# The MLP's up projection in seven products for eight, ahead of the whole down projection

## The chip, the cores and the metric

The kernel runs on one core of one Trainium2 chip, and the other cores are idle. The metric is the device time of one execution in microseconds. A core has TensorE (PE, matrix products out of SBUF into the eight banks of PSUM), VectorE (DVE, elementwise), ScalarE (ACT, elementwise functions of one operand), GpSimd (POOL, elementwise, no access to PSUM) and SyncE (SP, which issues the DMAs). Each engine works through its own queue in order, and semaphores tie the queues together.

## The reference

One layer of a decoder is computed for 544 tokens: a prompt of 512 and 8 samples of 4 new tokens. The width is 2048 and the MLP's hidden width 8192. All arrays are fp32.

```
x = x + concat(gla_part, att_part) @ w_out
h = rmsnorm(x, ffn_norm_w)
x = x + square(relu(h @ w_up)) @ w_down
y = rmsnorm(x, final_norm_w)
```

Ahead of this stand one combined projection, a gated linear attention, a dilated window attention, and the updates of their states. Only the output projection (`w_out`), the MLP (`w_up` of 2048 x 8192 and `w_down` of 8192 x 2048) and the last normalization matter here.

## The kernel before

Activations lie transposed, 128 features on the partitions and 544 tokens along the row, so that one tile `b` is 128 x 544. Matmuls take the tokens in two halves of 272 (`half`, L298). A matmul of this kernel runs in the reduced type fp32r, and full precision comes from splitting: every operand is a high part (rounded by ACT) and a low part (the remainder, a subtraction on DVE), and a product is three matmuls, high by high, high by low and low by high. For activations `put_x` (L367) makes the two parts, for weights `split_w` (L234): the tile `raw` of 128 x 1024 arrives by DMA, and each half of it, 128 x 512, becomes `wh` and `wl`. There are three buffers of each of `raw`, `wh` and `wl` (`NRAW`, `NWH`, L45).

The order of the work is the order of the program. The weights stand in one list `W`; `preps` is the list of the splits, and `prep_to` (L218) runs them some two or three steps ahead of the matmuls. `slot_main` (L1074) does one weight tile of 8 chunks: it starts the load of the tile three further on, splits, runs 48 matmuls into two banks and calls an evacuation. `defer` and `begin` (L317) put work at the start of a later slot, and `post` is a list of small pieces of work, of which one is run in each step.

The output projection has 32 slots. Behind each pair of them `evac_wo` (L1160) adds the residual, splits the scaled sum into the operand `X2` of the up projection and keeps its squares for the norm. Beside it run 32 updates of the recurrent state on DVE, one per slot (`start_upd`, L1200).

The MLP goes by eight groups of 1024 hidden features. A group's up projection is eight blocks of 128 features, each of two slots or 96 matmuls (16 chunks, three terms, two halves). `evac_up` (L1303) takes the relu and the factor of the norm out of PSUM on DVE, and ACT squares. The down projection of the first seven groups is already in the seven products of Winograd's form of Strassen's algorithm: the hidden blocks are combined into seven operands as they are made (`xops`, L1273), the weights into sums (`pair_preps`, L250; two of the four sums on POOL), and `down_pair` (L1324) runs seven products of 12 matmuls, each in a bank of its own out of eight, with ten additions on DVE into four running sums per pair of output blocks (`acc`). The next group's first up block is put between (`up_blocks`, L204). The last group's down projection is plain, 32 blocks of 24 matmuls, by halves of the tokens, with the last norm's squares beside it; `finish_acc` (L1351) turns the running sums into the result on POOL, during the last group's up projection.

Of the kernel before, what the change touches and what calls it, by code (L numbers as in the profile page):

```python
# [6 lines left out]
F32 = mybir.dt.float32  # L7
# [40 lines left out]
NSLOT3 = 9  # L48
SUMS = 5
# [72 lines left out]
def _body(ctx, nc, tc, A):  # L122
# [22 lines left out]
    def alloc(dt=F32):  # L145
        cnt[0] += 1
        n = f"b{cnt[0]}"
        for free, p, tag, bufs in tiers:
            if free[0]:
                free[0] -= 1  # L150
                t = p.tile([128, NTOK], dt, name=n, tag=tag, bufs=bufs)
                home[id(t)] = (t, free)
                return t
        raise SystemExit(f"no slots at {slot[0]}")
# [11 lines left out]

    def fix_done():
        fixctx.close()
        tiers.append(([NSLOT3], ctx.enter_context(tc.tile_pool(name="sb3", bufs=NSLOT3, side="right")), "blk3", NSLOT3))
# [29 lines left out]
    wo_seq = [(0, 0), (1, 0), (0, 1), (1, 1)]  # L199
    for nb in range(2, 16):  # L200
        wo_seq += [(nb, 0), (nb, 1)]
    for nb, hf in wo_seq:
        W.append(A["wout"][nb, hf])
    def up_blocks(g):  # L204
        """The up projections before group g's down projections: the next group's first one keeps TensorE busy while
        the operands of the last one are made."""
        return [(g, n) for n in range(g > 0, 8)] + ([(g + 1, 0)] if g < 7 else [])

    paired = set()
    for g in range(8):  # L210
        for g2, n in up_blocks(g):
            W += [A["wup"][g2 * 8 + n, hf] for hf in range(2)]
        if g < 7:
            paired.update(range(len(W), len(W) + 16, 2))
        W += [A["wdn"][g, nb % 16] for nb in range(32 if g == 7 else 16)]
# [18 lines left out]
    def split_w(key, r, eng):  # L234
        h = whm[key] = pool.tile([128, 4, 128], R32, name="wh%d_%d" % key, tag="wh", bufs=NWH)
        l = wlm[key] = pool.tile([128, 4, 128], R32, name="wl%d_%d" % key, tag="wl", bufs=NWH)
# [9 lines left out]
    def sum_tile():  # L246
        t = alloc()
        return t, t[:, :512].rearrange("p (c n) -> p c n", c=4)

    def pair_preps(i):  # L250
        """Weights of two blocks of output features, cut in halves by feature and by contraction, for the seven
        products of Winograd's form of Strassen's algorithm."""
        v = {}

        def a(r, q):
            return raws[i + r][:, 4 * q:4 * q + 4, :]

        def sm(k, x, y, op):
            t, v[k] = sum_tile()
            (G if SUMS >> (k - 1) & 1 else V).tensor_tensor(v[k], x, y, op=op)  # L260
            v[-k] = t

        def take(u, k):
            split_w((i, u), v[k], V)
            rel(v[-k])

        def u0():
            split_w((i, 0), a(0, 0), V)
            sm(1, a(1, 0), a(1, 1), OP.add)
            sm(2, v[1], a(0, 0), OP.subtract)  # L270

        def u1():
            split_w((i, 1), a(0, 1), V)
            sm(4, a(0, 1), v[2], OP.subtract)
            sm(3, a(0, 0), a(1, 0), OP.subtract)
            load_to(i + NRAW + 1)

        def u6():
            split_w((i, 6), a(1, 1), V)
            load_to(i + NRAW + 2)  # L280

        return [u0, u1, lambda: take(2, 4), lambda: take(3, 1), lambda: take(4, 3), lambda: take(5, 2), u6]

# [5 lines left out]
    while i < len(W):  # L289
        uidx[i] = len(preps)  # L290
        if i in paired:
            preps += pair_preps(i)
            i += 2
        else:
            preps += [lambda i=i: split_q(i, 0), lambda i=i: split_q(i, 1)]
            i += 1
# [852 lines left out]
    X2 = [None] * 16  # L1149
    xr = {}  # L1150

    def xr_load(nb):
        if nb < 16:
            xr[nb] = alloc()
            nc.sync.dma_start(xr[nb], A["xT"][nb])

    ss2 = alloc()
    r2 = alloc()

    def evac_wo(nb):  # L1160
        def f(pb):
# [3 lines left out]
            a, b = alloc(R32), alloc(R32)  # L1165
            put_x(a, b, t, nw[:, 16 + nb:17 + nb])
            X2[nb] = (a, b)
# [11 lines left out]
            defer(1, st_)  # L1179
        return f  # L1180
# [19 lines left out]
    def start_upd():  # L1200
# [5 lines left out]
        for k in range(32):  # L1206
            fetch, update, put = state_upd(k // 8, k % 8, *bufs[k % NUB])
            defer(k, fetch)
            defer(k + UD, update)
            defer(k + NUB - 1, put)  # L1210
        defer(31 + NUB, lambda: (rel(*own), fix_done()))

    xr_load(0)
    xr_load(1)
    wpb = {}
    base = n_in
    for s, (nb, hf) in enumerate(wo_seq):
        if hf == 0:
            wpb[nb] = mpair()
        if hf == 1 and nb == 0:  # L1220
            drain(lambda: all(n in GO for n in range(8)), gens)
            for n in range(8):
                put_go(n)
            defer(SUD, start_upd)
        slot_main(base + s, wpb[nb], Y, 8 * hf, hf == 0, hf == 1, evac=evac_wo(nb) if hf else None, nbg=2)
        if hf == 1:
            xr_load(nb + 2)
        elif nb == 0:
            pass
    for a, b in Y:  # L1230
        rel(a, b)
    base += len(wo_seq)
    begin()
    slot[0] += 1
    begin()

    acc = [alloc() for _ in range(16)]
    rel(GW["a"], GW["w"])

    x2t = {}  # L1240

# [4 lines left out]
    b0, b1 = balloc(), balloc()  # L1246
    r2done = [False]
    ah = [None] * 8
    perm = (0, 2, 4, 6, 1, 3, 5, 7)
    prev = {}  # L1250
    held = []
    xop = {k: [None] * 4 for k in ("B11", "B21", "B22", "T1", "T2", "T3", "T4")}

    def new_x():
        t = alloc(R32), alloc(R32)
        held.extend(t)
        return t

    def parts(names, j, src):
        t = new_x()  # L1260
        put_x(t[0], t[1], src)
        for hf, k in enumerate(names):
            xop[k][j] = (half(t[0], hf), half(t[1], hf))

    def first_op(j):
        a = prev["a"]
        if j % 2 == 0:
            prev["b"] = new_x()
        h, l = (half(t, j % 2) for t in prev["b"])
        xop["B11"][j] = (h, l)  # L1270
        post.append(lambda: put_x(h, l, half(a, 0)))

    def xops(n, a):  # L1273
        """The seven operands of a pair of hidden blocks (halves of the contraction) and the two halves of the tokens."""
        j = n // 2
        if n % 2 == 0:
            prev["a"] = a
            if n:
                first_op(j)
            return  # L1280
        a1, a2 = prev["a"], a

        def mix():
            ta = alloc()
            V.tensor_sub(half(ta, 0), half(a1, 1), half(a1, 0))
            V.tensor_sub(half(ta, 1), half(a2, 1), half(a1, 1))
            rel(a1)
            tb = alloc()
            V.tensor_sub(half(tb, 0), half(a2, 1), half(ta, 0))
            V.tensor_sub(half(tb, 1), half(a2, 0), half(tb, 0))  # L1290
            rel(a2)
            post.insert(0, lambda: (parts(("T2", "T4"), j, tb), rel(tb)))
            post.insert(0, lambda: (parts(("T1", "T3"), j, ta), rel(ta)))

        post.append(lambda: parts(("B21", "B22"), j, a2))
        post.append(mix)

    def split_a(n, t):
        ah[n] = (alloc(R32), alloc(R32))
        put_x(ah[n][0], ah[n][1], t)  # L1300
        rel(t)

    def evac_up(g, n):  # L1303
        def f(pb):
            if not r2done[0]:
                rms_r(r2, [ss2], D, (b0, b1))
                rel(ss2)
                brel(b0, b1)
                r2done[0] = True
            t = alloc()  # L1310
            for hf in range(2):
                V.scalar_tensor_tensor(half(t, hf), pb[hf][:, :HALF], 0.0, half(r2, hf), op0=OP.max, op1=OP.mult)
            S.activation(t, t, AF.Square)
            if g < 7 or n == 0:
                xops(n, t)
            else:
                split_a(n, t)
        return f

    # The sums kept are C11, C12 - C22, C21 - C22 and C22, to which the products go without sums of their own.  # L1320
    STEPS = (("B11", ((0, 0, 1), (1, 1, 1))), ("B21", ((0, 0, 1),)), ("B22", ((0, 1, 1),)),
             ("T1", ((1, 1, 1), (1, 0, 0))), ("T3", ((1, 1, 1), (0, 1, 0))), ("T2", ((1, 1, 1),)), ("T4", ((1, 0, 1),)))

    def down_pair(i, p):  # L1324
        for u, (x, outs) in enumerate(STEPS):
            if u % 3 == 0:
                begin()
# [237 lines left out]
```

## Time and profile before

| what | value |
|---|---|
| timed runs | 2416.05, 2418.59 and 2419.27 us, median 2418.59 |
| span of the profiled execution, first to last instruction | 2414.2 us |
| median less that span | 4.4 us |
| output projection, by the timeline | about 724 to 932 us |
| MLP, by the timeline | about 932 to 2399 us |
| DMA in the MLP | 104 GB/s |

The page of a profile gives busy times by engine, the chain of work that ended last, and groups of instructions by line. All of the kernel's instructions pass through one helper, so that the line is L94 nearly everywhere, and the names of the tiles tell them apart: `bank` is PSUM, `b` an activation tile (and here also a sum of weights), `raw`, `wh`, `wl` the weights. `out<-in` names what is written and read; `PEld` is TensorE's load of the stationary operand, one for each matmul. In a timeline a row has the start, the length, the engine, the operation, the count of instructions that it merges, and in brackets how long the engine was idle before and who released it. A row of a stretch has the busy time of each engine with its instructions, then the granted clock, the share of the DMA engines and GB/s.

### The profile page before, as it was taken

The page shows a single profiled execution, that of the slowest core. Times are in us where ns is not written, and L with a number is a line of the kernel's source. Part 1 is how long each engine was busy: PE and PEld are TensorE (multiplying, and loading weights), DVE is VectorE, ACT ScalarE, POOL GpSimd, SP SyncE. Part 2 cuts the span into 40 slices and gives each one's busy share as a digit, 9 for nine tenths or more (in the row PEclk, how much of TensorE's full clock was granted, in tenths as well). Part 3 has the DMA queues.
Part 4 walks back from the last instruction along what each step waited for, and adds up shares of the span by engine and source line. Part 5 has one row for each costly group of instructions (what it writes and reads, how often), then busy time and mean ns, then how long its engine had stood idle before and what let it go on. Part 6 is the DMA issues. An engine that isn't in the chain of part 4 may idle for free.

```text
span 2414.2 us, 47201 instructions
## 1 busy us (share of the span) xinstructions
PE 2383.4 (99%) x18836; PEld 2357.8 (98%) x18836; DVE 1776.7 (74%) x3589; ACT 911.7 (38%) x1680; POOL 564.2 (23%) x385
## 2 busy tenths in 40 slices
PE   9999999999999999999999999999999999999997
PEld 8999999999999999999999999999999999999997
DVE  6988888888876777476488488488487488488556
ACT  5332333332344323344333333333333333333365
POOL 3554544333431110021021021021021021022501
PEclk9999999999999999999999999999999999999999
DMA  6776765455525776223223223223223223223445
GB/s 231 272 261 246 261 230 183 174 192 191 176 82 170 265 262 229 88 84 103 89 86 105 88 87 107 89 86 106 89 89 106 89 86 107 90 85 123 144 157 179
DMA packets 116088, 355.30 MB, mean 147 GB/s; under 512 B 13051, under 2 KB 26363, under 8 KB 115868
## 3 DMA queue, kind: packets, MB, share of 16 engines
q1 hardware_dynamic: 114716, 351.18, 42.7%
q8 instruction: 147, 2.41, 0.4%
q10 hardware_dynamic: 1152, 1.11, 0.1%
q14 instruction: 73, 0.60, 0.1%
HBM read 334.02 MB, written 18.22 MB: 146 GB/s over the span
## 4 chain that ended last, share of the span: by engine, by line
PE 87%; DVE 8%; issue 2%; ACT 1%; DMA 1%; SPq 0%; DVEq 0%; ACTq 0%
PE bank L94 87%; DVE b L94 6%; DVE wl L94 1%; ACT b L94 1%; ACT wh L94 0%; DMA raw<-wup 0%; DVE AT L94 0%; DMA kv<-kcg 0%; DVE kv L94 0%; DMA b<-wglr 0%; DMA b<-xT 0%; DMA raw<-wdn 0%; DMA vtok<-s 0%; ACT L984 0%; DVE st L94 0%
## 5 line engine op out<-in xcount | busy, mean ns | idle before, releaser
L94 PE MATMUL bank<-b,wh 128*128 128x272 f32 x11648 | 1619.6, 288 | 2.8 <-ACT wh L94 1.4
L94 PEld LDWEIGHTS bank<-b,wh 128*128 128x128 f32 x11648 | 1522.1, 188 | 5.5 <-ACT wh L94 3.4
L94 PE MATMUL bank<-b,wl 128*128 128x272 f32 x5824 | 902.4, 291 | 0.0
L94 PEld LDWEIGHTS bank<-b,wl 128*128 128x128 f32 x5824 | 791.5, 189 | 8.7 <-issue 3.9
L94 ACT ACTIVATE wh<-raw 128x512 fp32r<-128x512 f32 x732 | 454.0, 627 | 624.1 <-PE bank L94 541.3
L94 DVE TENSOR_TENSOR wl<-raw,wh 128x512 fp32r<-128x512 f32 x552 | 411.5, 753 | 299.0 <-PE bank L94 205.2
L94 ACT ACTIVATE b<-b 128x544 f32<-128x544 f32 (+8 forms) x389 | 220.2, 572 | 412.0 <-DVE b L94 399.4
L94 POOL TENSOR_TENSOR wl<-raw,wh 128x512 fp32r<-128x512 f32 x180 | 270.6, 1509 | 384.3 <-ACT wh L94 330.2
L94 POOL TENSOR_TENSOR b<-raw 128x512 f32<-128x512 f32 x56 | 76.9, 1374 | 1095.6 <-ACT wh L94 628.1
L94 DVE TENSOR_TENSOR b<-b,b 128x272 f32<-128x272 f32 (+9 forms) x429 | 236.4, 574 | 38.3 <-ACT b L94 33.3
L94 DVE TENSOR_TENSOR wl<-b,wh 128x512 fp32r<-128x512 f32 x224 | 194.2, 867 | 35.6 <-ACT wh L94 35.0
L94 DVE TENSOR_TENSOR b<-b,bank 128x272 f32<-128x272 f32 x528 | 213.6, 427 | 1.9 <-PE bank L94 0.3
L94 ACT ACTIVATE wh<-b 128x512 fp32r<-128x512 f32 x224 | 135.1, 628 | 183.1 <-DVE b L94 129.6
L94 DVE SCALAR_TENSOR_TENSOR b<-bank,b 128x272 f32<-128x272 f32 (+1 forms) x228 | 90.7, 439 | 143.8 <-PE bank L94 135.5
L94 POOL TENSOR_TENSOR b<-b,b 128x544 f32<-128x544 f32 (+2 forms) x73 | 101.9, 1404 | 351.6 <-ACT b L94 293.3
L94 DVE SCALAR_TENSOR_TENSOR kv<-kv,b 128x320 f32<-128x320 f32 x256 | 159.2, 680 | 3.6 <-DMA kv<-vcg 3.6
L94 PE MATMUL bank<-b,b 128*128 128x272 f32 (+5 forms) x712 | 101.4, 311 | 6.0 <-ACT b L94 6.0
L94 DVE SCALAR_TENSOR_TENSOR b<-kv,b,b 128x320 f32<-128x320 f32 x126 | 100.1, 795 | 0.0
L94 POOL TENSOR_TENSOR b<-raw,raw 128x512 f32<-128x512 f32 x56 | 96.8, 1729 | 0.0
L94 PEld LDWEIGHTS bank<-b,b 128*128 128x128 f32 (+2 forms) x712 | 83.4, 177 | 12.1 <-ACT b L94 6.3
L94 DVE SCALAR_TENSOR_TENSOR b<-kv,b 128x320 f32<-128x320 f32 x126 | 93.5, 742 | 2.3 <-DMA kv<-kcg 2.2
L94 ACT ACTIVATE b<-bank 128x512 f32<-128x512 f32 (+5 forms) x114 | 44.6, 421 | 129.2 <-PE bank L94 101.7
(71 smaller groups left out, 749.5 us busy)
## 6 DMA issues: line engine op xcount, KB each, us to landing
raw<-wdn SPq DMA_DIRECT2D x144, 512.0 KB, 3.3
raw<-wup SPq DMA_DIRECT2D x128, 512.0 KB, 3.3
raw<-win SPq DMA_DIRECT2D x90, 512.0 KB, 4.8
kv<-kcg SPq DMA_DIRECT2D x64, 640.0 KB, 4.8
kv<-vcg SPq DMA_DIRECT2D x64, 640.0 KB, 4.9
raw<-wout SPq DMA_DIRECT2D x32, 512.0 KB, 5.8
b<-xT SPq DMA_DIRECT2D x32, 272.0 KB, 5.4
b<-vs SPq DMA_DIRECT2D x32, 256.0 KB, 5.1
```

The costliest lines, as they stand in the source:

```text
L94: return f(*a, **k)
```

## The change

The up projection goes into seven products as well, and the whole of it comes ahead of the down projection.

Operands of the up projection. The 16 blocks of its input are combined in pairs `j`, `j + 8` into seven operands per pair, each of half the tokens (`up_b2`, `up_b1`, `up_ta`, `up_tb`). To this end the output projection takes its blocks in the order 0, 8, 1, 9 and so on. The first three pairs of operands (`NEARLY = 3`) are made as `post` work during the output projection, the other five inside the first eight units of the up projection.

Units. The MLP is now a list of units of 12 matmuls. A pair of hidden blocks is seven products of two units; there are 32 pairs, and P4 of a pair stands behind P2 of the next. `run` prepares the weights two units ahead, then runs one piece of `post` or the unit's own `before`, the matmuls, and `after`. Weight tiles have seven buffers (`NRAW2 = 4` more), and `wh` and `wl` three as before. All sums of weights, four per seven products, are on DVE.

PSUM. Products that end in the same sum are accumulated in the same bank, one behind the other, and the bank is read in between where an intermediate sum is needed.

Hidden blocks. The relu moves to ACT and loses the factor of the norm, which is squared (`r2_calc`, in the second pair) and multiplied in at the end. The operands of the down projection are made from each pair at once and written to DRAM, seven tiles of 128 x 544 per pair (`spill`, issued three units later), and read back a group ahead, one per unit (`h_load`, `h_some`), or as many as there are free slots at the end of the up stage.

Down projection. Seven additions per pair in place of ten. `finish_acc` now also multiplies by the factor; two of its eight pairs stay on POOL, six go to DVE in the last group's first half. The state updates go four per three slots.

```diff
-NSLOT3 = 9
-SUMS = 5
+NRAW2 = 4
+NEARLY = 3
+HROOM = 5
+HROOM_U = 12
+FINP = 2
...
-            defer(k, fetch)
-            defer(k + UD, update)
+            defer(k * 3 // 4, fetch)
+            defer(k * 3 // 4 + UD, update)
...
+    def up_ta(j):
+        ta = mixed[j, 0] = alloc()
+        V.tensor_sub(half(ta, 0), half(xa[j], 0), half(xa[j], 1))
+        V.tensor_sub(half(ta, 1), half(xa[j + 8], 1), half(xa[j], 1))
+        two(XU, j, "ta", ta, ("P5", "P7"))
+        rel(xa.pop(j))
...
+    def run(us):
+        for u in us:
...
+            prep_to(FIRST + u.step + 3)
+            if u.before:
+                u.before()
+            elif post:
+                post.pop(0)()
+            u.mm()
+            if u.after:
+                u.after()
+            unit_no[0] += 1
...
+    ua = [bank[0], bank[1]]
+    ub, uc = [bank[2], bank[6]], [bank[3], bank[7]]
...
+        post.extend([mix_a, first, mix_b, put_a, put_2, put_b])
...
+    def up_after(p, k):
+        a, b, c = ua[p % 2], ub[p % 2], uc[p % 2]
...
+            if k == "P1":
+                copy("m1", halfb(a))
+                t = hid[p, 0] = alloc()
+                V.tensor_add(half(t, 0), halfb(b), half(tmp["m1"], 0))
+                rel(tmp.pop("m1"))
+            elif k == "P5":
+                copy("m5", halfb(c))
+            elif k == "P6":
+                copy("q", halfb(a))
+            elif k == "P3":
+                t = hid[p, 0]
+                V.tensor_add(half(t, 1), halfb(c), half(tmp["q"], 0))
+                rel(tmp.pop("q"))
+                S.activation(t, t, AF.Relu)
+                S.activation(t, t, AF.Square)
+            elif k == "P7":
+                t = hid[p, 1] = alloc()
+                V.tensor_add(half(t, 1), halfb(a), half(tmp["m5"], 0))
+                rel(tmp.pop("m5"))
+                S.activation(half(t, 1), half(t, 1), AF.Relu, scale=-1.0)
+            elif k == "P4":
+                t = hid[p, 1]
+                S.activation(half(t, 0), halfb(a), AF.Relu, scale=-1.0)
+                S.activation(t, t, AF.Square)
+                hidden_ops(p)
...
+            elif k == "P5":
+                add_w(("S2", q), sums["S1", q][1], quad(0, 0))
+                split_w(key, sums["S1", q][1], V)
+                drop(("S1", q))
...
+        useq.append((p, "P2"))
+        if p:
+            useq.append((p - 1, "P4"))
+        useq += [(p, k) for k in ("P1", "P5", "P6", "P3", "P7")]
...
+        return (lambda: [fs(j) for j in range(NEARLY, 8) if j // 4 == q]) if fs else None
...
+    dbank = {"P1": (0, True), "P2": (0, False), "P5": (1, True), "P4": (1, False), "P7": (2, True), "P3": (2, False),
...
+            add_acc(dst, ps, g == 0 and k in ("P1", "P2", "P3", "P4"), k == "P1")
...
+    D_ORDER = ("P1", "P5", "P2", "P6", "P7", "P4", "P3")
...
+        if p == 30 and k == "P3" and q == 0:
+            hq.extend(lambda j=j, i=i: h_load(0, j, i) for j, i in H_ORDER)
```

More of the change, by code (lines that the diff above doesn't have):

```diff
@@ L1230, in _body, with __init__ @@
[L1230 to L1238, printed above, removed]
-    x2t = {}
+            defer(k * 3 // 4, fetch)
+            defer(k * 3 // 4 + UD, update)
+            defer((k + NUB) * 3 // 4, put)
+        defer(35 * 3 // 4 + 1, lambda: (rel(*own), fix_done()))
+    FIRST = uidx[len(W) - 1] + 2
+    units = []
+    rawn = [0]
+    mraw = {}
+    class Unit:
+        def __init__(self, key, prep, mm, after=None, before=None):
+            self.key, self.prep, self.mm, self.after, self.before = key, prep, mm, after, before
@@ new lines, in sum_tile, with add_w, drop, add_unit @@
+    def sum_tile():
+        t = alloc()
+        return t, t[:, :512].rearrange("p (c n) -> p c n", c=4)
+    sums = {}
+    def add_w(key, x, y):
+        t, v = sum_tile()
+        V.tensor_add(v, x, y)
+        sums[key] = (t, v)
+    def drop(key):
+        rel(sums.pop(key)[0])
+    unit_no = [0]
+    def add_unit(u):
+        i = len(units)
+        u.step = i
+        units.append(u)
+        def prep():
+            raw_to(i)
+            u.prep()
+        preps.append(prep)
+    def product(key, ops, k, blocks, ps, start, stop):
+        def mm_():
+            n = len(blocks)
+            for w, o in ((whm, 0), (whm, 1), (wlm, 0)):
+                for c, j in enumerate(blocks):
+                    P.matmul(ps, w[key][:, c, :], ops[k][j][o], start=start and w is whm and o == 0 and c == 0,
+                             stop=stop and w is wlm and c == n - 1, skip_group_check=True)
+        return mm_
@@ new lines, in _body, with h_some @@
+    hq = []
+    hroom = [HROOM_U]
+    def h_some(n):
+        while n and hq and room() > hroom[0]:
+            hq.pop(0)()
+            n -= 1
+    D_ORDER = ("P1", "P5", "P2", "P6", "P7", "P4", "P3")
+    for g in range(7):
+        for p in range(8):
+            for i in range(2):
+                raw_seq.append((("d", g, p, i), A["wdn"][g, 2 * p + i]))
+            for k in D_ORDER:
+                n = len(units)
+                if k == "P6":
+                    raw_last["d", g, p, 0] = n
+                if k == "P4":
+                    raw_last["d", g, p, 1] = n
+                b_, st_ = dbank[k]
+                u = Unit((k, g, p), down_prep(g, p, k),
+                         product((k, g, p), XD[g], k, range(4), halfb(bank[4 * (p % 2) + b_]), st_, True),
+                         after=down_after(g, p, k))
+                add_unit(u)
@@ L1265, in first_op @@
[L1265 to L1318, printed above, removed]
@@ new lines, in _body, with freed @@
+    for a, b in Y:
+        rel(a, b)
+    begin()
+    slot[0] += 1
+    begin()
+    assert not later and not post
+    for u in units[:n_up]:
+        k, p, q = u.key
+        if p == 1 and k == "P2" and q == 0:
+            u.before = r2_calc
+        if p == 31 and q == 1:
+            def freed(u=u, k=k, after=u.after):
+                after()
+                for key in {"P1": ("b1",), "P3": ("a2",), "P7": ("ta",), "P4": ("tb",)}.get(k, ()):
+                    rel(*xtiles[key])
+                h_some(99)
+            u.after = freed
+        run([u])
+        if p == 30 and k == "P3" and q == 0:
+            hq.extend(lambda j=j, i=i: h_load(0, j, i) for j, i in H_ORDER)
@@ L1447, in _body @@
+    while hq:
+        hq.pop(0)()
+    for p in range(FINP):
+        finish_acc(p, G)
+    for u in units[n_down:]:
+        run([u])
     final_r(1)
@@ L1449, in _body @@
         final_out(1, nb)
-    assert base == len(W) and not later
+    assert not later and not later_u and not post
 def shape_consts():
```

515 lines of the change are left out of this document (335 added, 180 removed).

## The prediction, made before the result was known

> **What bounds the kernel now.** I read the page first, for the span, the busy shares and the chain that ended last.
>
> ```profile
> span 2414.2 us, 47201 instructions
> PE 2383.4 (99%) x18836; PEld 2357.8 (98%) x18836; DVE 1776.7 (74%) x3589; ACT 911.7 (38%) x1680; POOL 564.2 (23%) x385
> PE 87%; DVE 8%; issue 2%; ACT 1%; DMA 1%; SPq 0%; DVEq 0%; ACTq 0%
> ```
>
> TensorE (PE) is busy all the time and the chain runs over it. The three timed runs have a median of 2418.59 us, 4.4 us more than this span; I sum against the span and add 4.4. Then I cut the MLP out by stages, in busy times by stretch: the whole MLP, one up projection, one down projection.
>
> ```profile
> core 0: us, PE busy (x) PEld busy (x) DVE busy (x) ACT busy (x) POOL busy (x), PEclk, DMA share, GB/s
> 932.00:2400.00 1468.00, 1465.85 (x11626) 1460.80 (x11626) 1000.02 (x1812) 568.88 (x997) 227.90 (x157) 1.00 0.32 104
> 1133.00:1225.00 92.00, 92.00 (x736) 92.00 (x735) 43.58 (x77) 29.56 (x52) 3.00 (x2) 1.00 0.27 87
> 1229.00:1311.00 82.00, 82.00 (x650) 81.69 (x650) 78.50 (x147) 33.30 (x55) 21.64 (x14) 1.00 0.30 97
> ```
>
> In the up stage 736 matmuls take 92.00 us, so one starts every 0.125 us at full clock, and VectorE (DVE) is busy only 47% of the time. In the down stage, already in seven products, DVE is busy 96% and PE still loses nothing. So the time is a count of matmuls, as long as DVE and ScalarE (ACT) keep ahead. The up stage has the spare DVE time that a seven-product form would use. What it would use it for has prices in the timeline of one up block.
>
> ```profile
> 982.94 0.79 DVE L94 SCALAR_TENSOR_TENSOR b<-bank,b 128x272 f32<-128x272 f32 x2 [2.12 <-PE bank L94]
> 983.76 0.66 ACT L94 ACTIVATE b<-b 128x544 f32<-128x544 f32 x1 [4.08 <-DVE b L94]
> 984.33 0.61 ACT L94 ACTIVATE wh<-raw 128x512 fp32r<-128x512 f32 x1
> 984.85 0.65 ACT L94 ACTIVATE b<-b 128x544 fp32r<-128x544 f32 x1
> 984.97 0.69 DVE L94 TENSOR_TENSOR wl<-raw,wh 128x512 fp32r<-128x512 f32 x1 [1.25 <-ACT wh L94]
> 985.58 0.72 DVE L94 TENSOR_TENSOR b<-b,b 128x544 fp32r<-128x544 f32 x1
> 986.22 0.69 DVE L94 TENSOR_TENSOR wl<-raw,wh 128x512 fp32r<-128x512 f32 x1
> 986.82 0.43 DVE L94 TENSOR_TENSOR b<-b 128x272 f32<-128x272 f32 x1
> 987.17 1.26 DVE L94 TENSOR_TENSOR b<-b,b 128x272 f32<-128x272 f32 x3
> ```
>
> Starts of neighbours give what an operation costs its queue: on DVE 0.61 us for 128x512 (0.60 before a short one; I take 0.605), 0.64 for 128x544, 0.35 for 128x272; on ACT 0.57 for the square of 128x544. A waiting engine follows its releaser after 0.03 us (984.94 to 984.97).
>
> **The change part by part.** *Matmuls.* Up goes from 64 blocks of 96 matmuls (16 chunks, 3 terms, 2 halves) to 32 pairs of 7 products of 24: 6144 to 5376, so 768 fewer, **-96.0 us** at 0.125. The down products and the last group keep their counts. In the old up stage each weight tile is loaded for two neighbouring matmuls, in the new one for one; the down stage already does that, so its pitch is the test.
>
> ```profile
> 2195.17 1.16 PE L94 MATMUL bank<-b,wh 128*128 128x272 f32 x8
> 2205.80 1.17 PE L94 MATMUL bank<-b,wh 128*128 128x272 f32 x8
> ```
>
> One pair's 84 matmuls there take 10.63 us against 10.5 at 0.125, and this is a pair with DVE waits in the chain. No price for the loads.
>
> *The up loop.* A unit is now 12 matmuls, 1.5 us; a pair is 14 units, 21.0 us, in the order P2, P4 (of the pair before), P1, P5, P6, P3, P7. Per pair DVE gets 14 weight remainders and 8 weight sums of 128x512 (13.3 us), three adds out of PSUM and five small mixes of 128x272 (2.8) and three remainders of 128x544 (1.9): 18.0 us in 21.0. It fits on average, but not in order, because the work is bunched. P4 finishes the hidden blocks, and the next twelve or so DVE microseconds all sit behind it. I follow that loop once. PE runs P2 and P4, four units: 6.0. ACT then does Relu out of PSUM, Square, and only then the high part of P5's weights, since these stand behind in its queue.
>
> ```profile
> L94 ACT ACTIVATE b<-bank 128x272 f32<-128x272 f32 x32 | 11.7, 391 | 16.8 <-DVE b L94 12.7 <-PE bank L94 4.2
> L94 ACT ACTIVATE b<-b 128x544 f32<-128x544 f32 x7 | 4.6, 659 | 26.8 <-DVE b L94 26.8
> ```
>
> That is 0.08 + 0.39 + 0.03 + 0.57 + 0.61 + 0.03 = 1.71 (0.08 is the longer hop from a matmul, an estimate from the DVE start at 982.94 about that much after its last matmul). No Relu is in this trace: the first row, a copy of a half out of PSUM, stands for the one, and the Square's 0.66 for the one of a full tile. DVE then works without a pause through the remainders of P5, P6, P3 and P7 (8), the sums S2 to S4 that are left (5), mixes, first operand, P1's and P3's adds (7 of 128x272) and three 128x544: 13 x 0.605 + 7 x 0.35 + 3 x 0.64 = 12.2, and 0.1 until the last result is out. P3's add releases ACT: Relu 0.69, Square 0.57, then the high part of the next P2's weights 0.61, hops 0.08: 1.95. There PE starts the next pair. Sum 6.0 + 1.71 + 12.3 + 1.95 = **22.0 us per pair**, 1.0 over PE's own. I find the missing microsecond in two places: P3's second unit waits about 0.4 for its remainder, and the next P2 about 0.6 for ACT. From the second pair on, 31 x 1.0 = **+31 us**. Bounds: 0 if DVE's lag is absorbed by the three weight buffers, 50 (1.6 each) if each of the loop's 25 handovers costs 0.03 more than counted.
>
> *Shared banks.* Where a product adds to a bank, PE must wait until the earlier content is copied. In the up loop two units (3.0 us) lie between in each case, against an ACT copy of 0.39: nothing. In the down stage P1 and P2 share with one unit between, 1.5 us; the add after P1 starts 0.2 us late behind a sum and a remainder and takes 0.35: nothing, at worst 0.3 per pair, 17. DVE itself gets lighter there: 7 adds for 10, and 7 + 4 operations of 128x512 give 9.1 us in 10.5. The sums leave GpSimd, and these rows show what that sharing costs now:
>
> ```profile
> L94 DVE TENSOR_TENSOR wl<-b,wh 128x512 fp32r<-128x512 f32 x224 | 194.2, 867 | 35.6 <-ACT wh L94 35.0
> L94 DVE TENSOR_TENSOR wl<-raw,wh 128x512 fp32r<-128x512 f32 x30 | 21.5, 718 | 35.3 <-PE bank L94 26.1 <-ACT wh L94 8.8 <-issue 0.2
> ```
>
> The first is a mean beside GpSimd's sums, the second one of an up stage. Since PE did not wait in the down stage, this gains nothing: **0**.
>
> *Entry.* Today's entry costs half a microsecond:
>
> ```profile
> 931.81 0.79 DVE L94 TENSOR_TENSOR b<-bank,b 128x272 f32<-128x272 f32 x2 [1.37 <-PE bank L94]
> 932.40 2.41 PE L94 MATMUL bank<-b,wh 128*128 128x272 f32 x16 [0.50 <-DVE b L94]
> ```
>
> (-0.5.) In the new one only 3 of 8 operand sets are made during the output projection. The other five are made inside the first eight units, each time before the matmuls that need them, and each unit first needs the unit two ahead prepared, which waits for a buffer of the unit before. So nothing overlaps, and DVE's queue is the time: evacuation 0.8; eight sums and eight remainders 9.7; five of B2 at 0.64 and of B1 at 0.35, 5.0; five of Ta, where DVE makes two halves, waits for ACT's rounding (0.65) and subtracts: 0.35 + 0.43 + 0.03 + 0.65 + 0.03 + 0.64 = 2.13, 10.7; five of Tb, the same with the second half dependent on the first, 2.23, 11.2. Together 37.4, and about 0.5 for each unit's last matmuls, 4: 41 us, for 12.0 of matmuls: **+29**. Bounds 20 (handovers overlap, DVE ahead at the start) and 38 (first weights late as well). The r2 sums of squares move from the first evacuation to the second pair and still take four matmuls.
>
> *The clock.* Does a waiting PE lose clock? These rows say when.
>
> ```profile
> 316.72 0.78 PE L94 MATMUL bank<-cst,b 128*128 128x128 f32 x4 [1.80 <-DVE b L94]
> 317.97 2.37 PE L94 MATMUL bank<-b,wl 128*128 128x272 f32 x8
> 320.14 2.60 PE L94 MATMUL bank<-b,wh 128*128 128x272 f32 x16
> 316.00:320.00 4.00, 3.28 (x16) 2.96 (x17) 1.52 (x5) 1.19 (x4) 0.00 (x0) 0.71 0.91 323
> 723.94 2.28 PE L94 MATMUL bank<-b,wh 128*128 128x272 f32 x16 [1.19 <-ACT wh L94]
> ```
>
> After 1.80 us of idling the clock was 0.71 and eight matmuls took 2.37 us, some 1.2 more than the 1.17 of the down rows above, and the next sixteen 2.60; after 1.19 us of idling sixteen took 2.28. The entry has gaps of 2 us, the loop of 0.4 and 0.6. I add **+2** for the entry (0 to 5) and nothing for the loop. The Trainium skill, page "TensorE: Matmul & The Clock Gate", Part 1, puts the halved clock after an idle window of about 3.4 us; the trace shows it after a shorter gap, and by the page's window the entry would cost 0 to 2 and the sum be at most 2 us lower.
>
> *Up to down.* The operands come back from DRAM, 28 tiles of 272 KB for the first group. By count of free slots ten can be loaded before the last pair's P3 ends; the other 18 are issued at once then. The down stage wants the last of them 7 units later, P7, P4, P1, P5 and P2 between: 10.5 us. The rows:
>
> ```profile
> b<-xT SPq DMA_DIRECT2D x32, 272.0 KB, 5.4
> raw<-wdn SPq DMA_DIRECT2D x144, 512.0 KB, 3.3
> 10.00:20.00 10.00, 10.00 (x80) 10.00 (x79) 8.35 (x13) 9.07 (x17) 1.16 (x1) 1.00 1.05 406
> ```
>
> At 406 GB/s 18 such tiles take 12.3 us, after a first landing of some 3 us (the second row is a tile that meets no queue): 15, so **+5** (0 to 9, with two weight tiles ahead). On SP these loads wait for P3's matmuls, and behind them stand weights that seven buffers hold ahead. The Trainium skill, "DMA: Bandwidth & Descriptors", Specifications, gives an HBM limit of about 358 GB/s per core; this core alone reached 406 here, and by the page's figure the term would be some 1.7 us larger. Later groups load one tile per unit all along the stage before, and the last four arrive 6 units ahead of use: 0. Spills and weights in the up stage are 7 and 4 tiles, 4.0 MB per 22 us, 180 GB/s: hidden, on SP's queue as well, where a spill is issued three units after it is made.
>
> *Last group.* Six times, per two output blocks (6.0 us of matmuls), DVE, busy 65 of 96 us there now, also finishes two output blocks: four operations of 128x544 and two of 128x272, 3.3, beside its own 3.5. That is 0.8 over, 4.7 in all, of which the buffers hold about 2.7: **+2** (0 to 4.7). GpSimd does this today, hidden in the last up stage. The stage now:
>
> ```profile
> 2303.00:2399.00 96.00, 95.58 (x756) 95.23 (x755) 64.98 (x127) 65.23 (x126) 12.85 (x12) 1.00 0.53 177
> ```
>
> *Output projection.* The state updates run at 4 per 3 slots and three operand sets are added; one update is these two rows, 2.4 us.
>
> ```profile
> 937.69 0.35 DVE L94 TENSOR_SCALAR vtok<-vtok,dlS 128x256 f32<-128x256 f32 x1
> 938.07 2.05 DVE L94 SCALAR_TENSOR_TENSOR vtok<-ST,ktS,vtok 128x256 f32<-128x256 f32 x4
> ```
>
> Per slot of 6.0 us DVE has 1.2 for weights, 0.4 for the evacuation and 3.2 for updates, and 1.9 more over six slots: it lags at most 4 us, with two buffers of 3.0 ahead: 0 (to 4).
>
> Sum: -96.0 - 0.5 + 31 + 29 + 2 + 5 + 2 = **-27.5**. Span 2386.7, so with 4.4 about **2391 us**.
>
> **The rivals.** *A, the up loop stays bound by TensorE* (the lag is absorbed): -96.5 + 29 + 2 + 5 + 2 = -58.5, **2360**. For it: DVE at 96% cost PE nothing in the down stage. Against it: there every product had a bank of its own and no chain over ACT. *B, slower:* the two gaps of a pair, 0.4 + 0.6 in my sum, grow or merge past the limit between 1.19 and 1.80 us, and the clock falls once per pair, each time for some 1.6 us (1.2 on the eight matmuls, 0.3 to 0.4 on the next sixteen). From 0.9 us per pair on top of the loop's 1.0 it decides; at 1.6, 31 x 1.6 = 50 and the time is **2441**. For it: the longer gap may start the next; against: PE waits in two pieces, both under 1.19. *C, no change:* the loop at its upper price (+19), and the banks of the down stage at 0.15 per pair (+8) leave 0: **2418**. *D, the products save no time* because each matmul now brings its own weight load: refuted by the 10.63 us above, 1% at most.
>
> **How the numbers follow.** My forecast has 0.55 (2370 to 2408), A 0.17, B 0.16, C 0.11, D 0.01. The range leaves out part of A's and B's far ends: 2352 to 2434. A difference under 0.2%, 4.8 us, is about what a measurement of this kernel can tell from none. Faster: forecast and A, 0.72; same: 0.10; slower: B and the rest, 0.18.
>
> **What would show it.** Right: 10848 + 4 matmul records in the MLP; an up pair every 22.0 us and PE waits of about 0.4 and 0.6 us in it, named DVE wl and ACT wh; DVE busy 82% in the up stage and 87% in the down stage, where a pair stays at 10.5 us; some 29 us lost in the first eight units, and one wait for a DMA at the first down P6. Wrong: a pair of 21.0 us (A), a granted clock under 1.00 all through the up stage (B), waits of PE for DVE at P2 of every down pair (C).

## The result, and the profile after

The changed kernel takes 2480.9 us (median of four runs, 2478.7 to 2487.0), the kernel before beside it 2418.9 (2416.1 to 2420.4): a ratio of 1.026, with a 95% interval of 1.025 to 1.028. The forecast was 2391, with a range up to 2434. It is slower by 62 us, and by another stage than any that the rivals named. The page of the kernel after:

```profile
span 2481.3 us, 47598 instructions
PE 2350.5 (95%) x18068; PEld 2296.3 (93%) x18068; DVE 2006.8 (81%) x4042; ACT 1121.3 (45%) x2096; POOL 373.2 (15%) x253
PE 42%; DVE 10%; ACT 4%; issue 3%; DMA 1%; DVEq 0%; ACTq 0%; SPq 0%
```

The 768 matmuls are gone (18836 before), but PE is no longer on the chain for most of the span (42% for 87%). The stages, cut at the same matmuls in the two timelines:

| stage | before | after | difference | forecast |
|---|---|---|---|---|
| up to the output projection | 723.9 | 728.2 | +4.3 | same code; 723.7 to 727.4 in all other runs |
| output projection | 208.0 | 273.7 | **+65.7** | 0 (to 4) |
| MLP | 1467.2 | 1465.2 | -2.0 | -27.5 |
| final norm | 15.0 | 14.2 | -0.8 | 0 |
| span | 2414.2 | 2481.3 | +67.1 | -27.5 |

The projection whose matmuls the change only puts in another order loses as much as the whole kernel does. Busy times of four stretches after: output projection, entry of the up stage, up loop, down stage.

```profile
725.00:940.00 215.00, 181.02 (x1301) 177.69 (x1299) 138.55 (x255) 64.63 (x109) 22.74 (x16) 0.91 0.62 191
1000.00:1060.00 60.00, 34.80 (x162) 29.22 (x161) 34.41 (x64) 21.60 (x39) 1.34 (x1) 0.66 0.12 45
1120.00:1180.00 60.00, 58.57 (x451) 56.60 (x450) 49.01 (x88) 36.00 (x68) 0.00 (x0) 1.00 0.61 194
1900.00:1960.00 60.00, 60.00 (x480) 60.00 (x480) 52.78 (x103) 25.30 (x40) 0.00 (x0) 1.00 0.49 161
```

In the first row DVE is busy 64%, so the amount of its work is not the bound. In the last, a stretch of the down stage is as forecast, no loss, with DVE at 88%. What SP waited for while the output projection ran, in the kernel before and then after (in total, times, longest; L1180 is the fetch of a state, L1191 and in the kernel before L1195 the store):

```profile
SPq L1195 <- DVE vtok L94: 33.8, 14, 4.3
SPq L1177 <- DVE b L94: 31.3, 16, 12.6
SPq L1195 <- DVE b L94: 24.5, 10, 4.2
```

```profile
SPq L1180 <- DMA gs<-b: 74.8, 14, 7.3
SPq L1170 <- DVE b L97: 34.3, 5, 12.6
SPq L1180 <- DMA gs<-vtok: 33.9, 7, 6.6
```

New are 21 waits, 109 us, of a fetch for a stored state (`gs`) to land. One of them in the timeline after, with all engines:

```profile
951.30 0.43 SPq L222 DMA_DIRECT2D raw<-wout  x1
951.83 0.39 SPq L1191 DMA_DIRECT2D gs<-b  x1
957.69 1.15 ACT L97 ACTIVATE wh<-raw 128x512 fp32r<-128x512 f32 x2 [10.64 <-DMA raw<-wout]
957.96 0.33 SPq L1180 DMA_DIRECT2D b<-s  x1
958.35 0.90 SPq L1183 DMA_DIRECT2D b<-vs  x2
958.38 3.99 PE L97 MATMUL bank<-b,wh 128*128 128x272 f32 x16 [5.51 <-ACT wh L97]
959.34 0.38 SPq L222 DMA_DIRECT2D raw<-wout  x1
```

A buffer's state is stored at 951.83. The next state goes into the same buffer, so SP issues nothing more until 957.96, and the weight tile for the slot three further on is behind it, at 959.34. PE waits 5.5 us for the tile before, and is then at half clock for 16 matmuls (3.99 us; 2.2 is usual). The fetches of the 21 slots with such a wait go out from 781.66 to 966.85, 20 rounds of 9.26 us; a slot has 6.0 us of matmuls. 20 times 3.26 is 65 us, the whole loss. What PE waited for in the output projection after:

```profile
PE bank L97 <- ACT wh L97: 43.0, 15, 5.5
```

That is the high part of a weight tile. For remainders out of DVE it waited 1.7 us, once, and DVE waited for no state. The other 23 of the 65.7 us are matmuls at a slower pace behind the waits: the clock of the stretch is 0.91.

Why the wait is new: before, update k was stored in slot k + 3, and the next fetch into its buffer went out in slot k + 4. After, both stand in slot (k + 4) * 3 // 4. With four buffers and a faster pace the slot between was lost, and the update's own distance of two slots (`UD = 2`) filled what was left. **Theory 1**: SP waits for the store's landing, and the weight loads stand behind it. Rivals: **2**, the pace and the operand sets are too much for DVE; **3**, the DMA bandwidth is used up.

### The profile page after: what moved, and what is told of

Its sections match the earlier page's. It is cut to its first block, busy times and chain, and to the rows that moved or that the text cites. A ratio compares the mean times of both kernels' runs of the same rounds, so it can differ in the third digit from the quotient of the medians.

```text
span 2481.3 us, 47598 instructions
## 1 busy us (share of the span) xinstructions
PE 2350.5 (95%) x18068; PEld 2296.3 (93%) x18068; DVE 2006.8 (81%) x4042; ACT 1121.3 (45%) x2096; POOL 373.2 (15%) x253
## 4 chain that ended last, share of the span: by engine, by line
PE 42%; DVE 10%; ACT 4%; issue 3%; DMA 1%; DVEq 0%; ACTq 0%; SPq 0%
PE bank L97 42%; DVE b L97 5%; DVE wlP L97 4%; ACT b L97 2%; ACT whP L97 2%; DVE wlL L97 0%; DMA b<-hs 0%; DMA b<-hl 0%; DMA raw<-wdn 0%; DVEq L97 0%; ACTq L97 0%; ACT whL L97 0%; DVEq L1841 0%; SPq L1577 0%
## 5 line engine op out<-in xcount | busy, mean ns | idle before, releaser
L97 PE MATMUL bank<-b,whP 128*128 128x272 f32 x6720 | 996.9, 290 | 45.1 <-ACT b L97 26.0
L97 PEld LDWEIGHTS bank<-b,whP 128*128 128x128 f32 x6720 | 903.7, 190 | 58.9 <-ACT b L97 30.7
L97 PE MATMUL bank<-b,wh 128*128 128x272 f32 x3904 | 546.9, 294 | 43.3 <-ACT wh L97 43.0
L97 PE MATMUL bank<-b,wlP 128*128 128x272 f32 x3360 | 568.5, 291 | 6.6 <-DVE wlP L97 2.5
L97 PEld LDWEIGHTS bank<-b,wh 128*128 128x128 f32 x3904 | 519.6, 193 | 47.5 <-ACT wh L97 47.2
L97 PEld LDWEIGHTS bank<-b,wlP 128*128 128x128 f32 x3360 | 475.9, 190 | 20.9 <-DVE wlP L97 20.8
L97 DVE TENSOR_TENSOR wlP<-b,whP 128x512 fp32r<-128x512 f32 x480 | 331.2, 695 | 46.5 <-ACT whP L97 41.9
L97 PE MATMUL bank<-b,wl 128*128 128x272 f32 x1952 | 302.5, 298 | 1.7 <-DVE wl L97 1.7
L97 PEld LDWEIGHTS bank<-b,wl 128*128 128x128 f32 x1952 | 267.0, 192 | 7.8 <-issue 3.9
L97 ACT ACTIVATE wh<-raw 128x512 fp32r<-128x512 f32 x244 | 148.5, 622 | 252.0 <-DMA raw<-wout 131.6
```

Source lines behind the costliest of these rows:

```text
L97: return f(*a, **k)
```

## The experiments

Times are medians. The kernel before was run beside each and took 2417.8 to 2420.2 us.

**Store one slot earlier** (e1), in the kernel after:

```diff
-UD = 2
+UD = 1
-            defer((k + NUB) * 3 // 4, put)
+            defer((k + NUB) * 3 // 4 - 1, put)
```

> The kernel after, with the store of an updated state one slot ahead of the next fetch into its buffer (as in the kernel before), and the update one slot after its own fetch to make room; pace, operand sets and all else as they are. Theory 1 (SP issues the fetch behind the store of the same buffer and waits for its landing, and the weight loads of the output projection stand behind it): the waits of SP for the stored states (109 us in 21 waits) go under 15 us, the output projection takes 208 to 216 us in place of 274, the time is 2412 to 2424 us. Rival 2 (the faster pace, four updates per three slots, with the operand sets loads DVE too much): the output projection stays over 255 us, the time over 2460. Rival 3 (DMA bandwidth): the same bytes in the same time, so no change, 2475 to 2487.

2424.4 us, 56.5 less. Of SP's waits of a fetch for a stored state one is left, of 0.4 us, and the stretch looks like this:

```profile
725.00:940.00 215.00, 205.86 (x1613) 204.31 (x1614) 164.68 (x305) 75.45 (x128) 28.58 (x19) 0.99 0.72 243
```

The same pace, the same sets, more bytes per second (243 for 191 GB/s): rival 3 falls, and rival 2 as the main cause. The output projection takes 219.9 us, 12 more than before, where I had expected at most 8.

**Store one slot later** (e2), in the kernel before:

```diff
-            defer(k + NUB - 1, put)
+            defer(k + NUB, put)
```

> The kernel before, pace of one update per slot, with the store of the state one slot later, in the slot of the next fetch into the same buffer; nothing else. Theory 1: the same wait appears on SP once in each of 28 slots, at the 3 to 7 us that it has in the kernel after, and the output projection grows by 20 to 70 us from 208; the time is 2438 to 2488 us. Rivals 2 (pace and operand sets on DVE) and 3 (DMA bandwidth): nothing changes, 2414 to 2424.

2475.5 us, a ratio of 1.024 (1.022 to 1.026) from one `- 1`. The same lines appear:

```profile
SPq L1184 <- DMA gs<-b: 74.3, 14, 7.0
SPq L1184 <- DMA gs<-vtok: 73.7, 14, 6.4
```

The fetches from 782.03 to 974.70 are 23 rounds of 8.38 us, 2.38 over a slot, 55 us; measured 57.7. Of these the output projection takes 48.5, and most of the rest are two waits in the first two slots of the MLP, 3.5 and 3.7 us, with the lower clock behind them. So the distance from store to fetch costs the kernel after its 57 us, and would have cost the kernel before the same.

**Six buffers, update two slots behind its fetch** (e9), to see where the remaining 12 us come from. `NUB = 6`, two states more in the idle `vtok`, three tiles more, and `- 1` as in e1.

> The kernel after with six state buffers for four, so that an update stays two slots behind its fetch (as in after) and the store still goes one slot ahead of the next fetch into its buffer. The run with one slot between fetch and update left 12 us of the output projection (219.9 us for 208), in seven waits. If these came from updates that waited for their fetch: 208 to 213 us, time 2411 to 2418. If they come from two updates in one slot (the pace of four per three), which stand ahead of the weights' remainders on DVE: 217 to 223 us, time 2420 to 2428.

2426.4 us, output projection 219.8: the 12 us do not come from updates that wait for their fetch. With the update two slots behind the fetch, as in the kernel after, the store's slot alone again takes the loss away.

**No operand sets in the output projection** (e12), e1 with `NEARLY = 0`:

> The first experiment with no operand sets made in the output projection (all eight in the first units of the up stage). If the sets on DVE are what is left of the output projection's loss (219.9 for 208): 208 to 212 us there. If it is the pace of the updates: 216 to 221. The entry has three more sets: by its queue 3 times (0.64 + 0.35 + 2.13 + 2.23) = 16 us longer, so that the time is 2428 to 2444 us.

2433.5 us; the output projection takes 208.9, so the rest came with the sets, a true part of rival 2. That it is DVE's share of their work, and not ACT's, was not tried alone. The entry takes 75.4 for 58.6 in e1: a set costs 5.6 us there and 3.7 in the output projection.

**The way from the wait to PE.** The state's transfers on GpSimd's queue (e8), then e1 with that (e11); `nc.sync.dma_start` becomes `nc.gpsimd.dma_start` in fetch and put:

> The kernel after, with the state's fetches and stores issued by GpSimd in place of SP; same slots, same bytes, same waits of a fetch for the store's landing, only on another engine's queue. Theory 1 (what costs is that the weight loads stand behind the waiting fetch on SP): the output projection takes 208 to 216 us, the time is 2412 to 2424. Rival (the wait itself, by making the update late and so DVE): the output projection stays over 240 us, time over 2445. Rival (bandwidth): no change.

> The first experiment (store one slot ahead of the next fetch, update one slot behind its fetch) with the state's transfers on GpSimd's queue. With the queue alone changed, the output projection still took 262 us, GpSimd waiting 89 us for the stores' landing and DVE some 45 us for the states fetched late. If that wait was the cause there too: it is gone, the output projection takes 208 to 222 us, time 2412 to 2427. If GpSimd's queue is itself what made the fetches late (0.5 us for each issue, its own additions between): over 235 us, time over 2440.

2467.1 and 2461.9 us, output projections of 261.7 and 257.2. In e8 theory 1's number missed and that of the first rival came, and in e11 that of the slow queue. In e8 PE waits 24.7 us, in 10 waits, for remainders out of DVE and 12.9, in 7, for high parts; in the kernel after it was 1.7 and 43.0. What GpSimd, DVE and PE waited for in e11:

```profile
POOL b L97 <- ACT b L97: 139.2, 15, 33.6
...
DVE b L97 <- DMA b<-s: 23.4, 7, 7.4
DVE vtok L97 <- DMA vtok<-s: 20.2, 5, 7.0
...
PE bank L97 <- DVE wl L97: 29.3, 11, 5.9
```

GpSimd's additions for the norm wait for ACT's squares, which exist only when PE and DVE have finished a block. Now the fetches stand behind them, arrive late, DVE waits in the update, and the weights' remainders wait on DVE. So late states cost PE by a second way, over DVE, and these two runs do not test the first, over the weight loads on SP. That the kernel after goes the first way is read from its waits above.

**The weight load ahead of the fetch** (e14), kernel after, in the output projection:

```diff
+        if i >= n_in:
+            load_to(i + NRAW)
         begin()
         load_to(i + NRAW)
```

> The kernel after, with the next weight tile of the output projection issued at the head of a slot, ahead of the due store and fetch, in place of behind them; the fetch still waits for the store's landing, in the same slots. Theory 1 as it stands (weights behind the waiting fetch on SP are what TensorE waits for): the load goes out up to 8 us earlier, the output projection takes 208 to 240 us in place of 274, time 2412 to 2450. Rival (SP is simply out of time: with 5 to 7 us of waiting in a slot of 6 us, whatever the order, the next load comes as late, or the late states hold DVE): over 255 us, time over 2460.

2472.0 us, output projection 262.4: the rival's number. SP's queue in this run:

```profile
944.05 0.43 SPq L222 DMA_DIRECT2D raw<-wout  x1
944.58 0.63 SPq L1193 DMA_DIRECT2D gs<-b  x1
950.46 0.33 SPq L1182 DMA_DIRECT2D b<-s  x1
950.85 0.90 SPq L1185 DMA_DIRECT2D b<-vs  x2
951.85 0.37 SPq L1106 DMA_DIRECT2D b<-xT  x1
952.32 0.38 SPq L222 DMA_DIRECT2D raw<-wout  x1
```

A round is still 8.3 us from load to load: 5.9 from the store to the fetch that waits for its landing, and some 2.4 for the issues. So SP holds one whole landing in every slot and is itself the bound. But the edit changes only the slot in which a load is counted: on the queue the order is load, store, fetch, load, as in the kernel after, so this run does not show that the order is of no account. Store, load, fetch was not tried. It might shorten the wait, since the store lands just behind the weight tile issued ahead of it: in the kernel after the tile releases ACT at 957.69 and the store releases the fetch at 957.96. The Trainium skill, "DMA: Bandwidth & Descriptors", Anatomy of one DMA, a section on GpSimd's path, says that a semaphore wait of a transfer happens on the issuing sequencer, ahead of its dispatch. The trace agrees for SP: the gap from 944.58 to 950.46 is such a wait.

**The up loop's order** (e3, e7). In `run`, the next weights are split ahead of `after`; e3 does it for all up products, e7 for two:

```diff
             u.mm()
             if u.after:
+                if u.step < n_up and u.key[0] in ("P3", "P4"):
+                    prep_to(FIRST + u.step + 4)
                 u.after()
```

> The kernel after, with the splitting of the next weights put ahead of the work that a product's end releases (copies, Relu, Square, the adds out of PSUM) in the up units; the output projection's loss stays in. Theory of the prediction (the high part of the weights stands behind Relu and Square in ACT's queue, which costs 1.0 to 1.7 us twice per pair): a pair of the up loop goes from 22.34 to 21.0 to 21.5 us, the time by 26 to 41 us to 2440 to 2455. Rival (DVE's bunched work behind P4 is what holds, ACT's order matters nothing): 22.1 us or more, the time over 2472.

> As the run with the weights first, but only behind P3 and P4, where Relu and Square stand; the copies out of PSUM go ahead of the weights as in the kernel after. In the run with all of them weights first a pair took 21.87 us, with one wait of 0.4 to 0.6 us per pair for a copy out of PSUM. Theory (that wait was made by the new order itself: the copy stands behind a high part which waits for DVE's sum): the wait goes, a pair takes 21.0 to 21.5 us, the time is 2445 to 2458 us. Rival (DVE's bunched work is the bound, and whatever stands last pays): 21.7 to 22.1 us per pair, 2460 to 2473.

2463.2 and 2445.2 us, 18 and 36 less than after; e3 lies between its two numbers, e7 has its theory's. Where PE waits in a pair, in the kernel after, in e3, and e7's stretch of the loop:

```profile
1196.41 1.27 PE L97 MATMUL bank<-b,whP 128*128 128x272 f32 x8 [0.33 <-ACT whP L97]
1211.59 1.16 PE L97 MATMUL bank<-b,whP 128*128 128x272 f32 x8
1212.82 0.78 PE L97 MATMUL bank<-b,wlP 128*128 128x272 f32 x4
1218.75 1.26 PE L97 MATMUL bank<-b,whP 128*128 128x272 f32 x8 [0.33 <-ACT whP L97]
```

```profile
1205.96 1.27 PE L97 MATMUL bank<-b,whP 128*128 128x272 f32 x8 [0.25 <-ACT b L97]
1227.82 1.27 PE L97 MATMUL bank<-b,whP 128*128 128x272 f32 x8 [0.46 <-ACT b L97]
```

```profile
1120.00:1180.00 60.00, 60.00 (x477) 59.55 (x476) 51.02 (x94) 39.02 (x74) 0.00 (x0) 1.00 0.59 186
```

In the kernel after a pair takes 22.34 us, 1.34 over its matmuls. By the starts of the matmuls P2 loses 0.6 for ACT's high part (`whP`), and each of P3's two units 0.34 for a remainder out of DVE (`wlP`): the eight matmuls from 1211.59 take 1.23 to the next start, 1.00 is usual. In e3 a pair takes 21.86, with one wait at P7 for a copy out of PSUM (`ACT b`). In e7 it takes 21.2, and no wait over 0.1 us stands from 1120 to 1660. DVE does the same work, 51 us in 60, and a pair now loses 0.2: the loss was the order. The edit moves the weights ahead on ACT and on DVE alike, so it does not show which of the two queues counts.

**The entry's order** (e4). In the first twelve units the operands are made ahead of later weights, and the mixes of set j + 1 are issued before the remainder of set j:

```diff
-            prep_to(FIRST + u.step + 3)
+            if u.step >= 12:
+                prep_to(FIRST + u.step + 3)
             if u.before:
                 u.before()
...
+                    if i + 1 < len(js):
+                        mix(js[i + 1])
+                    put(j)
```

> The kernel after, with the first twelve up units making their operands ahead of the splitting of later weights, and the mixes of one operand set issued ahead of the remainders of the set before, so that DVE does not wait for ACT's rounding; same operations. Theory of the prediction (DVE's queue is the time of the entry, and 0.65 us of ACT in each of ten mixed sets and the waits for weight buffers are part of it): the first twelve units take 42 to 47 us in place of 57.9, the time 2465 to 2470. Rival (the clock, 0.66 there, sets the time of the units, since the gaps stay over 2 us): 53 us or more, the time 2475 to 2482.

2463.1 us; the twelve units take 43.2 for 57.9, as expected. The total moved 3 more: in the two traces the last three pairs of the loop take 2.6 less and the output projection 2.8 less, of which I show no cause. The clock is 0.66 from 1000 to 1040 as the rival had it, but PE's gaps behind the first, 2.26 us, are under 2, so the clock did not hold the units.

**Finishing the sums** (e5 on GpSimd in the seventh down group, e10 on DVE one operation at a time):

> The kernel after, with the finishing of the running sums (four operations of 128x544 and two of 128x272 per two output blocks) on GpSimd behind each pair of the seventh group of the down stage, where the pair is complete, in place of six pairs on DVE inside the last group; the residuals they add are loaded there too. Theory (DVE's 0.8 us too much per two blocks is the last group's loss, 7.5 us): the last group takes 95.5 to 97.5 us in place of 103.8, the down stage loses under 2 us, the time is 2471 to 2477 us, by the run shown of after. Rival (GpSimd at work beside DVE slows DVE, busy 88% in the down stage, and the last down group pays): the last group is faster but the seventh down group longer by as much, time within 2 us of after.

> The kernel after, with the finishing of the running sums of six pairs still on DVE in the last group's first half, but cut into single operations, five for four units, in place of six at once ahead of every fourth unit. With GpSimd doing it in the seventh down group the time did not fall, because DVE's remainders grew from 0.78 to 1.08 us beside it. Theory (the bunch is the loss: DVE has 28 us of its own and 20 us of finishing in 48 us of matmuls, so spread out it just fits): the last group takes 96 to 99 us in place of 103.8, time 2473 to 2478 us by the run shown of after. Rival (the sum of the work is the loss): 102 us or more, no change.

e5: 2489.9 us, 9 more than after, outside both numbers; the rival's mechanism came, at a higher price. The last group is shorter (98.0 for 103.8) but the down stage 15.0 longer. One group of DVE's remainders of 128x512, from 2220 us to shortly before the last group, first after, then e5, and PE in e5:

```profile
L97 DVE TENSOR_TENSOR wlP<-b,whP 128x512 fp32r<-128x512 f32 x52 | 40.3, 775 | 0.0
```

```profile
L97 DVE TENSOR_TENSOR wlP<-b,whP 128x512 fp32r<-128x512 f32 x49 | 52.9, 1080 | 0.0
```

```profile
2289.50 1.24 PE L97 MATMUL bank<-b,whP 128*128 128x272 f32 x8 [1.42 <-DVE b L97]
2294.74 1.24 PE L97 MATMUL bank<-b,whP 128*128 128x272 f32 x8 [0.50 <-DVE b L97]
2302.98 1.24 PE L97 MATMUL bank<-b,whP 128*128 128x272 f32 x8 [1.42 <-DVE b L97]
```

A pair takes 13.5 us there for 10.5. The products that wait for DVE are P3 (1.42) and the next pair's P2 (0.50): each shares a bank with the product two units ahead, P7 and P1. e10: 2477.4 us (2475.1 to 2478.9), last group 98.8: the bunch was most of that loss, though the total is hardly outside the spread of after (from 2478.7).

**Together** (e13: e1, e7, e4 and e10; e15: with e14's order too):

> What helped, together: the store one slot earlier (57 us measured), the weights first behind P3 and P4 (36), the entry's order (18) and the finishing spread over the last group (expected 3 to 8). If the parts add up: 2480.9 - 57 - 36 - 18 - 5 = 2365 us, range 2355 to 2375, faster than the kernel before (2418) by 2%. If they share a cause (each makes DVE wait less, so that the next limit shows): 2380 to 2400.

> The combined kernel (2373 us, output projection 222 us) with the same order of loads. There the fetch no longer waits, and what is left is put down to DVE's load by the operand sets: then the order matters little, 2368 to 2376 us. If loads behind stores that wait for a late update are part of what is left, the output projection goes to 208 to 214 us and the time to 2358 to 2366.

e13 takes 2373.3 us (2370.0 to 2376.3), 0.981 of the kernel before (0.979 to 0.982); the four parts alone are 113.5 us, together 107.6: they nearly add up. e15 takes 2370.0 (2368.8 to 2374.0), ratio 0.980 (0.979 to 0.982); its spread overlaps e13's, so the load's order is not shown to help. Left are 14 and 10 us in the output projection and some 24 in the entry.

## Why the prediction was wrong, point by point

- **Output projection, "it lags at most 4 us ... 0 (to 4)": this step failed.** Of the 94.6 us that the span was off, 65.7 are here and 25.5 in the MLP. The step added up DVE's time per slot and looked at nothing else that the new slot numbers move. Of three expressions that changed, fetch, update and store, it did not put in numbers for one buffer: k = 4 is fetched in slot 3, and update 0 of the same buffer is stored in slot 3. The price was in the trace of before, had I looked for it there: a store's landing, 4.8 and 2.4 us in the median of its two groups, which after became 6.0 and 5.9. With one slot between store and fetch 53.8 of the 65.7 are gone (e1). The lag that I had priced, the sets' work, is 11 of the 12 us that e1 leaves (219.9 for e12's 208.9), near three times the bound of 4.
- **Matmuls, -96:** right, 768 fewer. But the MLP before was not without loss: 11616 matmuls at 0.125 are 1452 us, of 1467.2; I had taken 0.5 of these 15.
- **The up loop, +31:** mechanism right, size too small. The two places are the ones forecast: 0.6 at P2 for ACT, and P3's remainders, 0.34 in both of its units where I had 0.4 in the second. So 28 pairs take 22.34 in place of 22.0, with DVE busy 82% as forecast. From 1059.8 to 1765.9 us the loop loses 52 over its matmuls, beyond the bound of 50: 1.34 in each of 28 pairs, 38, then 4 in each of the last three, which take 25 us, and 1.2 ahead of the last P4. These three pairs make the last group's operands, with multiplication and remainder in one piece; that this piece is the cause was not tried. e7, in which the next weights no longer stand behind Relu and Square, takes the loss of a pair from 1.34 to 0.2; so the two chains of the working, 1.71 and 1.95, were made by the order. I had not drawn the conclusion that the order is free to choose.
- **Entry +29 and clock +2:** measured 39.8. The two pitches that I had worked out are there, 2.15 for 2.13 and 2.34 for 2.23:

```profile
1028.65 0.59 PE L97 MATMUL bank<-b,whP 128*128 128x272 f32 x1 [1.56 <-ACT b L97]
1030.80 0.59 PE L97 MATMUL bank<-b,whP 128*128 128x272 f32 x1 [1.56 <-ACT b L97]
...
1043.52 0.60 PE L97 MATMUL bank<-b,whP 128*128 128x272 f32 x1 [2.37 <-ACT b L97]
1045.86 0.60 PE L97 MATMUL bank<-b,whP 128*128 128x272 f32 x1 [1.74 <-ACT b L97]
```

  The missing 9 lie between them. There ACT waits 8.9 us (5 times) for PE to give back a weight buffer, and PE is near half clock (0.50 to 0.58 from 1018 on). I had counted 0.5 per unit for the last matmuls, at full clock, and 2 in all for the clock. Which of the two makes the 9 was not separated; e4 takes 14.7 us away at the same clock.
- **Up to down, +5 (0 to 9):** in its range, but only 1.0 us is for its reason, a DMA at the first P6. Another 1.6 are at the first P2, which waits for ACT's copy out of the bank it shares with P1 and which I had put at nothing. At its end the stage waits 2.5 beside GpSimd's finishing, also for a shared bank; it loses 9 in 597, and nearly nothing between.
- **Last group, +2 (0 to 4.7):** 7.8, beyond the bound. The buffers did not hold 2.7: four finishings cost PE 1.1 each behind `DVE wlL`, and one 0.4. e10 gets 5.0 of the 7.8 back; of the rest I show no cause.
- **The rivals:** A was possible, e7's loop is nearly that, but not this kernel's. B is refuted: the clock is 1.00 from 1060 to 1660, and 0.97 in the 120 us behind, where the last three pairs are. Of C the loop at its upper price came (52 for 50), the banks in every pair of the down stage did not; D did not come. That the slower side had a chance at all is luck: what made the kernel slower was in no rival.

In sum the MLP gave -2 for -27.5. With the store a slot earlier the kernel is 0.3% slower than before (e1), and with the orders changed as well 1.9% faster (e13).

## What to carry to other kernels

When a pace or a buffer count changes, write down for one buffer the slots of fetch, update, store and next fetch, in numbers, and keep a slot between store and fetch: when an issuing queue has to sit out a landing in every slot, the landing sets the length of the slot (8.3 to 9.3 us here, for 6.0 of matmuls), and putting the load ahead in the program gave back only 11 of 66 us (e14). Price a moved step on each queue that it stands in, not on the busiest engine alone. Where an engine with time to spare is late, first exchange the order of two pieces of work; that was worth 36 us here for two lines.

## What the runs showed of the hardware

- GpSimd's additions beside DVE lengthened a remainder of 128x512 on DVE from 0.78 to 1.08 us on average (e5), and single ones from 0.68 to 1.85:

```profile
2283.24 5.21 POOL L97 TENSOR_TENSOR b<-b,b 128x544 f32<-128x544 f32 x3
2287.53 1.48 DVE L97 TENSOR_TENSOR wlP<-b,whP 128x512 fp32r<-128x512 f32 x1
...
2291.43 0.68 DVE L97 TENSOR_TENSOR wlP<-b,whP 128x512 fp32r<-128x512 f32 x1
```

  The Trainium skill, "SBUF — State Buffer", SBUF: two separate sides, says that the two share a port pair which one of them holds for a whole instruction. The trace agrees: the last of the three GpSimd additions ends at 2288.45, and the long remainder 0.56 us behind it, at 2289.01. From 2215 to 2372 us in e5 all 35 remainders that took over 0.8 us end 0.55 to 0.56 us behind a GpSimd operation, whenever they had begun.
- The length of a gap alone does not tell whether the clock falls. After 1.77 us of waiting 16 matmuls took the usual 2.27 us, and after 3.45 they took 3.66 (kernel after):

```profile
946.58 2.27 PE L97 MATMUL bank<-b,wh 128*128 128x272 f32 x16 [1.77 <-ACT wh L97]
...
976.20 3.66 PE L97 MATMUL bank<-b,wh 128*128 128x272 f32 x16 [3.45 <-ACT wh L97]
```

  In e14 they took 2.27 after 3.03, and in e8 3.30 after 2.17. So the limit between 1.19 and 1.80 us in the prediction was read from too few rows.
